# Gates and output projections of a second block by tokens, and a wide first FFN product, in an ordered two-block kernel

## The chip, the cores and the metric

One core of one Trainium2 chip runs the whole program. The metric is the device time of one execution in microseconds (us), the median over several runs.

## The reference

Two blocks of a network on 256 tokens of width 1024, in fp32. The first block (a state-space mixer, a latent attention, a convolutional FFN) is not touched but by the order of its instructions. The second block, cut to what matters:

```python
def second_block(x, ...):
    h = _rmsnorm(x, norm1_g)
    proj = h @ w_in                       # 1024 -> queries, keys, values, gates
    ... g_ma, g_mb = split(proj)          # 2 x 1024 gate columns, last in w_in
    y_a = _nsa_mixer(...)                 # 256 x 768: compressed, selected, window attention
    y_b = _dilated_mixer(...)             # 256 x 256
    mixed = sigmoid(g_ma) * (y_a @ w_o_a) + sigmoid(g_mb) * (y_b @ w_o_b)
    x = x + mixed @ w_out
    h2 = _rmsnorm(x, norm2_g)
    return x + jnp.square(jax.nn.relu(h2 @ w_up)) @ w_down   # 1024 -> 4096 -> 1024
```

Inside `_nsa_mixer`, `_compress` multiplies blocks of keys and of values (45 rows each) with two 2048x256 weights, 4 MB in all.

## The kernel before

**Products.** Each fp32 operand is split into a high part (a copy of type fp32r) and a low part (the rest), and a product is three matmuls that add up in PSUM: high x high, high x low, low x high. The helper's comments don't name it, so: in tile names `h` and `l` at the end are these parts. Weights stream from HBM in blocks of up to 128x2048. `need` (L319) issues for each half of a block a DMA on SyncE's queue into `wraw` (3 buffers), a ScalarE copy to `whi` and a VectorE subtraction to `wlo` (5 buffers each).

There are two forms of product. `pairB` (L502, with `mmB` L481) works by channels: a 128x128 weight is the stationary operand, the 256 tokens move, and the result has channels on the partitions; one matmul has 256 columns, a PSUM tile `pb` holds two channel blocks. `chunkA` (L491, with `mmA` L470) works by tokens: 128 tokens of the activation are stationary, 384 or 512 columns of weight move, the result `pa` has tokens on the partitions, one PSUM tile for each half of the tokens. Both take their PSUM from the tag `acc` (3 banks).

**Activations.** The stationary side needs channels on the partitions, so after each norm `norm_T` scales the rows (`xn` on VectorE) and `gain_T` (L423) transposes them on TensorE, 128x128 at a time, into a bank `trn`, two token halves per bank, and splits each bank into high and low with the gain as a scale (ScalarE, then VectorE). `late_T` (L442) does the same without the row scale, which is applied later. `spread` (L457) turns a column of row scales into a row `rrow` across channels, with two transposes `trr`.

**Second block.** In `block2` (L1291) the order of the text is: norm and transposes, the input product by tokens, queries and keys, compression (`kps` times `cw` weights into `ph`, 64 matmuls of 256 columns for keys and for values together, and the low parts `wlo` on 45 rows), attention, then the gates: eight `pairB` tiles, times `rrow` on VectorE, tanh on ScalarE (`tg`). Then `oa` (L1707): four `pairB` tiles over the 768 columns of `yAT`, gated into `mixA`; then `ob` over `yBT`, gated into `mixB`, added, and split into `mixT`. `out` is a product by tokens. The last FFN is 16 `pairB` tiles `up2`, relu on ScalarE (`r2`), square on VectorE (`u2`), split into `uT`, and two `chunkA` products over `uT` into the output.

**Order.** Nothing runs in the order of the text. `_Plan` (L655) records every operation, estimates its time with `_cost` (L575), simulates the engines and queues (a DMA by three constants) and picks what comes next on each engine by a rank: the table `RANK` (L41) gives each stage one number or one for each of its parts. A replay (L637) then issues everything in the order found, all from one line, L652 in the profile. So a change of a cost moves instructions everywhere, in the first block too.

```python
        if eng == "D":
            return max(150.0, 1.422 * n)
...
                elif e == "D":
                    end = now + 475.0
                    link = max(link, now + 1100.0) + ops[i][1][e]
                    fin = link + 700.0
```

Of the kernel before, what the change touches and what calls it, by code (L numbers as in the profile page):

```python
# [10 lines left out]
F32R = mybir.dt.float32r  # L11
# [6 lines left out]
P = 128  # L18
# [27 lines left out]
    "gate": [19.55, 0.24, 0.53, 11.34, -1.8, 19.33, 8.91, 19.47], "mix": [30],  # L46
    "in2": [39.8, 45.14, 45.06, 55.07, 49.45], "cmp": [40.9], "nsa": [41.09, 41.19, 49.84], "qb": [46.71, 41.14],
    "kb": [45.22, 46.76], "vb": [40.89, 41.09], "dil": [60.1, 50.29, 45.27, 41.14],
    "gate2": [46.76, 60, 62.18, 59.1, 60, 60.05, 45.57, 54.81], "mix2": [70, 70, 70, 71, 72], "ffn2": [80]}
PASSES = 3  # L50
# [26 lines left out]
def _weights():  # L77
# [33 lines left out]
    for nm, c0, n in A2_CHUNKS:  # L111
        for i in range(2):
            add((nm, i), 4 * n, "w_in_2", lambda w, i=i, c0=c0, n=n: _blk(w, range(4 * i, 4 * i + 4), [(c0, n)]))
        if nm == "qa1":
            for kv in "kv":
                for i in range(2):
                    add(("cw", kv, i), 2048, "cmp_%s_w1_2" % kv, lambda w, i=i: _blk(w, range(8 * i, 8 * i + 8), [(0, 256)]))
    for i in range(8):
        add(("g2", i), 2048, "w_in_2", lambda w, i=i: _tiles(w, (2 * i, 2 * i + 1), range(8), GA2))
    for i in range(4):  # L120
        add(("oa", i), 1536, "w_o_a_2", lambda w, i=i: _tiles(w, (2 * i, 2 * i + 1), range(6)))
    add(("ob", 0), 2048, "w_o_b_2", lambda w: _tiles(w, range(8), range(2)))
    for n in range(2):
# [18 lines left out]
def _cut(key, w):  # L142
    return 768 if key[0] == "mla" else w // 2

# [138 lines left out]
def _body(plan, x_in, wts, cst, out):  # L283
# [35 lines left out]
    def need(key):  # L319
        o, w = woff[key]  # L320
        src = wts[o:o + P * w].rearrange("(p n) -> p n", p=P)
        cut = _cut(key, w)
        parts = []
        plan.block = key
        for a, b in ((0, cut), (cut, w)):
            raw = plan.tile("wts", [P, 1024], F32, "wraw", "wraw", WRAW)
            plan.fetch = len(plan.ops)
            DQ.dma_start(raw[:, :b - a], src[:, a:b])
            hi = plan.tile("wts", [P, 1024], F32R, "whi", "whi", WHL)
            lo = plan.tile("wts", [P, 1024], F32R, "wlo", "wlo", WHL)  # L330
            A.activation(hi[:, :b - a], raw[:, :b - a], AF.Copy)
            V.tensor_tensor(lo[:, :b - a], raw[:, :b - a], hi[:, :b - a], op=OP.subtract)
            parts.append((a, hi, lo))
        plan.block = None
        return parts

    def wsl(w, o, n):
        a, hi, lo = w[1] if o >= w[1][0] else w[0]
        return hi[:, o - a:o - a + n], lo[:, o - a:o - a + n]
# [82 lines left out]

    def gain_T(xs, gain, name):  # L423

        res = hl(name, 4)
        for k in range(8):
            ps = ps_tr("trn")[:, :T]
            for tt in range(NTT):
                PE.transpose(ps[:, tt * P:(tt + 1) * P], xs(tt, k), ident)
            split((res[k // 2][0][:, k % 2], res[k // 2][1][:, k % 2]), ps, gain[:, k:k + 1])  # L430
        return res
# [9 lines left out]

    def late_T(x, gain, name):  # L442

        plan.rank, back = ("first", 0), plan.rank
        res = gain_T(lambda tt, k: x[:, tt, k * P:(k + 1) * P], gain, name)
        plan.rank = ("norm", 0)
# [78 lines left out]
class _Plan:  # L525
# [49 lines left out]
    def _cost(eng, op, outs, ins):  # L575
# [3 lines left out]
        if eng == "D":  # L579
            return max(150.0, 1.422 * n)  # L580
        if eng == "PE":
# [11 lines left out]
        if op == "tensor_tensor_reduce":  # L593
            outs = outs[:1]
        if eng == "A":
            return 0.833 * n + (51.0 if psum else 93.0) + 93.0 * (ptr + len(outs) - 1)
        fast = op in ("tensor_scalar", "tensor_copy", "memset") and not psum
        return (0.52 if fast else 1.042) * n + 68.0 + 61.0 * ptr

# [105 lines left out]
    def _run(self, graph, seq):  # L705
# [29 lines left out]
        while done < n:  # L735
# [23 lines left out]
            for e in ENGS:  # L759
# [45 lines left out]
                elif e == "D":  # L805
                    end = now + 475.0
                    link = max(link, now + 1100.0) + ops[i][1][e]
                    fin = link + 700.0
                else:
# [481 lines left out]
def block2(env, x2):  # L1291
# [31 lines left out]
    V.tensor_scalar(rnh, rn, 0.5, None, op0=OP.mult)  # L1323
    rrow = S.spread(rnh)

# [120 lines left out]
    for kv in range(2):  # L1446
        kps = []
        pos = C("pos" + "kv"[kv])
        for s0 in range(4):
# [7 lines left out]
            kps.append(t)  # L1457
        for i in range(2):
            w = S.need(("cw", "kv"[kv], i))
            for j in range(8):  # L1460
# [6 lines left out]
                if last:  # L1467
                    PE.matmul(ph[:90, c], both, wh, start=False, stop=True)
    hp = a2("hp")[:90]
    S.copy(hp, ph[:90])  # L1470
# [163 lines left out]
    for hp in range(2):  # L1634
# [28 lines left out]
        for i in range(2):  # L1663
# [3 lines left out]
            for b, n in enumerate((384, 512, 256)):  # L1667
                tt = min(b, 1)
                S.copy(prob[i][b][:, :n], prob[i][b][:, :n], rd[:, tt:tt + 1])
        pTs = []  # L1670
        for g in range(3):
            pT = S.pt_tile("pT3")
            o = (g % 2) * 256
            for i in range(2):
# [3 lines left out]
                S.copy(pT[:, i], pt[:, :384])  # L1678
            pTs.append(pT)
        po = ps_o("pob")[:, :T]  # L1680
        S.plan.group = ("pob", hp)
        for g in range(3):
            for kb in range(2):
                for i in range(2):
                    hd = 4 * g + 2 * hp + i
                    PE.matmul(po[64 * i:64 * i + 64, kb * P:], vb[hd // 6][kb][:, (hd % 6) * 64:(hd % 6) * 64 + 64],
                              pTs[g][:, i, 2 * kb * P:(2 + kb) * P], start=g == 0 and kb == 0, stop=g == 2 and kb == 1)
        S.plan.group = None
        S.split((yBT[0][0][:, hp], yBT[0][1][:, hp]), po)


    tg = []
    for i in range(8):
        S.rank("gate2", i)
        ps = S.pairB(("g2", i), hT)
        t = a2("tg").rearrange("p (a b) -> p a b", a=2)
        V.tensor_tensor(t, ps, rrow[:, None, :].to_broadcast([P, 2, T]), op=OP.mult)
        A.activation(t, t, AF.Tanh)
        tg.append(t)
    mixA = []  # L1700
    for i in range(4):
        S.rank("mix2", i)
        ps = S.pairB(("oa", i), yAT, 6)
        t = a2("mixA").rearrange("p (a b) -> p a b", a=2)
        V.scalar_tensor_tensor(t, tg[i], 1.0, ps, op0=OP.add, op1=OP.mult)
        mixA.append(t)
    mixT = S.hl("mixT", 4)  # L1707
    S.rank("mix2")
    w = S.need(("ob", 0))
    for i in range(4):  # L1710
        ps = S.ps_acc("pob2").rearrange("p (a b) -> p a b", a=2)
        for m in range(2):
            S.mmB(ps[:, m], yBT, w, 2, lambda k: ((2 * i + m) * 2 + k) * P)
        t = a2("mixB").rearrange("p (a b) -> p a b", a=2)
        V.scalar_tensor_tensor(t, tg[4 + i], 1.0, ps, op0=OP.add, op1=OP.mult)
        V.tensor_tensor(t, t, mixA[i], op=OP.add)
        S.split(mixT[i], t)
    x3 = x2
# [8 lines left out]
    S.rank("ffn2")  # L1727
    hT, ms = S.late_T(x3, C("g_n2"), "hT")
    rsq = small("rsq", 2)
    V.reciprocal(rsq, ms)  # L1730
    uT = S.hl("uT", 16)
    for i in range(16):
        ps = S.pairB(("up2", i), hT)
        t = a2("u2").rearrange("p (a b) -> p a b", a=2)
        r = a2("r2").rearrange("p (a b) -> p a b", a=2)
        A.activation(r, ps, AF.Relu)
        V.tensor_tensor(t, r, r, op=OP.mult)
        S.split(uT[i], t)
# [42 lines left out]
```

## Time and profile before

| | |
|---|---|
| median of 3 runs | 995.23 us (994.27 to 995.67) |
| own time of the profiled execution | 995.55 us |
| its span in the trace | 993.8 us |
| mean granted TensorE clock | 0.993 of full speed |
| HBM read | 164.18 MB, 166 GB/s over the span |

The span runs from the first to the last recorded instruction; 1.75 us of the execution's own time lie around it. TensorE is PE in the rows (its weight loads PEld), VectorE DVE, ScalarE ACT, SyncE SP. A row's duration of a pipelined matmul overlaps that of the next, so what one costs is read from start to start, or from the length of a chain of many. `A<-B,C` means that tile A is written from B and C.

### The profile page before, as it was taken

The numbers are of one execution on the slowest core, as the hardware profiler recorded it, in microseconds if no ns is written. First come the engines' busy times: TensorE is split into PE (matmuls) and PEld (weight loads), VectorE is DVE, ScalarE is ACT, GpSimd is POOL, SyncE is SP. The second block draws the span as 40 slices with busy tenths as digits, with TensorE's granted clock in tenths as the row PEclk, the third lists the DMA queues.
The fourth block names the chain that finished last, engine by engine and source line by source line (L and its number), as shares of the span: only waits on it lengthen the run. The fifth ranks groups of instructions, "written<-read, shape, count | busy, mean of one in ns | idle before, by whom it ended". The sixth has DMA issues, their size and how long they took to land.

```text
span 993.8 us, 18122 instructions
## 1 busy us (share of the span) xinstructions
PE 979.3 (99%) x6737; PEld 906.7 (91%) x6737; DVE 787.0 (79%) x1841; ACT 615.2 (62%) x1233; POOL 0.2 (0%) x4
## 2 busy tenths in 40 slices
PE   9999999999999999999999998999999999999998
PEld 7899988999999899999988997998889989998886
DVE  6887999999787779989954999999877866665442
ACT  6665889877554566666653666867676455554341
POOL 0000000000000000000000000000000000000000
PEclk9999999999999999999999998999999999999999
DMA  7655644344455555555565555534323556555561
GB/s 253 221 168 163 211 128 164 101 132 156 148 172 180 174 181 185 187 178 186 186 198 158 172 167 188 186 114 131 125 91 113 183 181 198 178 182 187 188 218 64
DMA packets 50537, 166.44 MB, mean 167 GB/s; under 512 B 5617, under 2 KB 6929, under 8 KB 50321
## 3 DMA queue, kind: packets, MB, share of 16 engines
q1 hardware_dynamic: 50448, 165.28, 51.3%
q8 instruction: 53, 0.87, 0.4%
q14 instruction: 36, 0.29, 0.1%
HBM read 164.18 MB, written 1.08 MB: 166 GB/s over the span
## 4 chain that ended last, share of the span: by engine, by line
PE 88%; DVE 5%; DMA 4%; ACT 2%; issue 1%; SPq 0%; DVEq 0%; ACTq 0%
PE pb L652 46%; PE pa L652 28%; DMA wraw<-in_wts_dram 4%; DVE wlo L652 2%; PE trp L652 2%; PE py L652 1%; ACT whi L652 1%; PE po L652 1%; PE psS L652 1%; PE pob L652 1%; PE pq L652 1%; PE trq L652 1%; PE pov L652 1%; PE pk L652 1%; PE psN L652 1%
## 5 line engine op out<-in xcount | busy, mean ns | idle before, releaser
L652 DVE TENSOR_TENSOR wlo<-wraw,whi 128x1024 fp32r<-128x1024 f32 (+3 forms) x318 | 368.2, 1161 | 160.0 <-ACT whi L652 156.4
L652 ACT ACTIVATE whi<-wraw 128x1024 fp32r<-128x1024 f32 (+3 forms) x318 | 320.9, 1010 | 276.2 <-PE pb L652 146.2
L652 PE MATMUL pb<-hTl,whi 128*128 128x256 f32 x1056 | 302.3, 287 | 0.0
L652 PE MATMUL pb<-hTh,wlo 128*128 128x256 f32 x1056 | 302.2, 287 | 0.0
L652 PE MATMUL pb<-hTh,whi 128*128 128x256 f32 x1056 | 301.6, 286 | 0.0
L652 PEld LDWEIGHTS pb<-hTl,whi 128*128 128x128 f32 x1056 | 203.6, 193 | 2.1 <-issue 1.9
L652 PEld LDWEIGHTS pb<-hTh,wlo 128*128 128x128 f32 x1056 | 203.7, 193 | 1.3 <-issue 1.0
L652 PEld LDWEIGHTS pb<-hTh,whi 128*128 128x128 f32 x1056 | 203.6, 193 | 1.0 <-issue 0.8
L652 PE MATMUL pa<-whi,uTh 128*128 128x512 f32 x216 | 84.2, 390 | 0.0
L652 PE MATMUL pa<-whi,uTl 128*128 128x512 f32 x216 | 84.2, 390 | 0.0
L652 PE MATMUL pa<-wlo,uTh 128*128 128x512 f32 x216 | 84.2, 390 | 0.0
L652 PE MATMUL pa<-whi,hTh 128*128 128x384 f32 (+2 forms) x224 | 80.5, 361 | 0.0
L652 PE MATMUL pa<-whi,hTl 128*128 128x384 f32 (+2 forms) x224 | 79.7, 356 | 0.0
L652 PE MATMUL pa<-wlo,hTh 128*128 128x384 f32 (+2 forms) x224 | 79.4, 355 | 0.0
L652 PEld LDWEIGHTS pa<-whi,uTl 128*128 128x128 f32 x216 | 40.6, 188 | 8.5
L652 PEld LDWEIGHTS pa<-wlo,uTh 128*128 128x128 f32 x216 | 40.6, 188 | 8.3
L652 PEld LDWEIGHTS pa<-whi,uTh 128*128 128x128 f32 x216 | 40.6, 188 | 8.2
L652 PEld LDWEIGHTS pa<-whi,hTh 128*128 128x128 f32 x224 | 42.2, 189 | 2.3 <-issue 0.3
L652 PEld LDWEIGHTS pa<-whi,hTl 128*128 128x128 f32 x224 | 42.1, 188 | 2.3 <-issue 0.3
L652 PEld LDWEIGHTS pa<-wlo,hTh 128*128 128x128 f32 x224 | 42.2, 189 | 2.0 <-issue 0.2
L652 PE MATMUL pb<-ysTh,wlo 128*128 128x256 f32 x128 | 37.0, 289 | 0.0
L652 DVE SCALAR_TENSOR_TENSOR fcv<-fpr,call,fcv 128x254 f32<-128x254 f32 (+1 forms) x88 | 36.6, 478 | 0.3 <-ACT fcv L652 0.3
(396 smaller groups left out, 1724.6 us busy)
## 6 DMA issues: line engine op xcount, KB each, us to landing
wraw<-in_wts_dram SPq DMA_DIRECT2D x250, 512.0 KB, 4.2
wraw<-in_wts_dram SPq DMA_DIRECT2D x52, 384.0 KB, 3.2
dec<-aD SPq DMA_DIRECT2D x16, 256.0 KB, 5.9
wraw<-in_wts_dram SPq DMA_DIRECT2D x8, 256.0 KB, 2.7
wraw<-in_wts_dram SPq DMA_DIRECT2D x4, 448.0 KB, 4.4
wraw<-in_wts_dram SPq DMA_DIRECT2D x4, 420.0 KB, 3.9
call<-in_cst_dram SPq DMA_DIRECT2D x1, 1076.5 KB, 9.1
out_dram<-yo SPq DMA_DIRECT2D x3, 256.0 KB, 4.0
```

Source lines behind the costliest of these rows:

```text
L652: getattr(engines[eng], op)(*[swap(a) for a in args], **{k: swap(a) for k, a in kw.items()})
```

## The change

The gates become four `chunkA` products of 512 columns; tanh reads PSUM directly with the row scale as its scale operand, so `rrow` and its `spread` go. `ob` and `oa` become `chunkA` products per half of the output columns; the gated sum `mixB` has tokens on the partitions and is turned by 16 transposes `trm`, two channel blocks per bank, then split into `mixT`. In the last FFN, `gain_T` keeps each of the eight channel blocks as one tile with the high part beside the low part; a high weight then multiplies both in one matmul of 512 columns, and the low weight multiplies the high part in one of 256, into PSUM tiles `pu` of another tag (`g`, 5 banks). ScalarE or VectorE copies the second half to `l2`, VectorE adds it to the first (`u2`) and does relu and square in one operation. In `gain_T` two channel blocks share a bank: four transposes, then two splits. The `pob` matmuls of the dilated attention stand with their group's transposes instead of after all groups. In the planner the constants of a DMA and of half-height operations change, and some ranks.

```diff
-    "gate2": [46.76, 60, 62.18, 59.1, 60, 60.05, 45.57, 54.81], "mix2": [70, 70, 70, 71, 72], "ffn2": [80]}
+    "gate2": [46.76, 60, 60, 54.81], "mix2": [70, 70.2, 70.1, 71, 72], "ffn2": [80]}
...
-            return max(150.0, 1.422 * n)
+            return max(150.0, 1.8 * n)
...
+        half = 115.0 if n >= 256 and outs[0].ap[0][1] == 64 else 0.0
...
-                    end = now + 475.0
-                    link = max(link, now + 1100.0) + ops[i][1][e]
-                    fin = link + 700.0
+                    end = now + 430.0
+                    link = max(link, now + 1000.0) + ops[i][1][e]
+                    fin = link + 1060.0
...
         for k in range(8):
-            ps = ps_tr("trn")[:, :T]
-            for tt in range(NTT):
-                PE.transpose(ps[:, tt * P:(tt + 1) * P], xs(tt, k), ident)
-            split((res[k // 2][0][:, k % 2], res[k // 2][1][:, k % 2]), ps, gain[:, k:k + 1])
+            if k % 2 == 0:
+                pair = ps_tr("trn").rearrange("p (a b) -> p a b", a=2)
+                for tt in range(NTT):
+                    for j in range(2):
+                        PE.transpose(pair[:, j, tt * P:(tt + 1) * P], xs(tt, k + j), ident)
+            ps = pair[:, k % 2]
+            dst = (res[k][:, 0], res[k][:, 1]) if beside else (res[k // 2][0][:, k % 2], res[k // 2][1][:, k % 2])
+            split(dst, ps, gain[:, k:k + 1])
...
-    rrow = S.spread(rnh)
...
-        ps = S.pairB(("g2", i), hT)
-        t = a2("tg").rearrange("p (a b) -> p a b", a=2)
-        V.tensor_tensor(t, ps, rrow[:, None, :].to_broadcast([P, 2, T]), op=OP.mult)
-        A.activation(t, t, AF.Tanh)
-        tg.append(t)
...
+    for n in range(4):
+        S.rank("gate2", n)
+        ps = S.chunkA([("g2", n, 0), ("g2", n, 1)], hT, 512, 4)
+        tg.append([a2("tg") for _ in range(NTT)])
+        for tt in range(NTT):
+            A.activation(tg[n][tt], ps[tt], AF.Tanh, scale=rnh[:, tt:tt + 1])
+    mixT = []
+    for n in range(2):
+        S.rank("mix2", n)
+        mix = [a2("mixB") for _ in range(NTT)]
+        ps = S.chunkA([("ob", n)], yBT, 512, 2)
+        for tt in range(NTT):
+            V.scalar_tensor_tensor(mix[tt], tg[2 + n][tt], 1.0, ps[tt], op0=OP.add, op1=OP.mult)
+        ps = S.chunkA([("oa", n, 0), ("oa", n, 1)], yAT, 512, 3)
+        for tt in range(NTT):
+            t = a2("mixA")
+            V.scalar_tensor_tensor(t, tg[n][tt], 1.0, ps[tt], op0=OP.add, op1=OP.mult)
+            V.tensor_tensor(mix[tt], t, mix[tt], op=OP.add)
+        S.rank("mix2", 2 + n)
+        mixT += S.hl("mixT", 2)
+        for i in range(2):
+            pt = ps_tr("trm").rearrange("p (a b) -> p a b", a=2)
+            for j in range(2):
+                for tt in range(NTT):
+                    PE.transpose(pt[:, j, tt * P:(tt + 1) * P], mix[tt][:, (2 * i + j) * P:(2 * i + j + 1) * P], ident)
+            S.split(mixT[2 * n + i], pt)
...
-        ps = S.pairB(("up2", i), hT)
         t = a2("u2").rearrange("p (a b) -> p a b", a=2)
-        r = a2("r2").rearrange("p (a b) -> p a b", a=2)
-        A.activation(r, ps, AF.Relu)
-        V.tensor_tensor(t, r, r, op=OP.mult)
+        l = a2("l2").rearrange("p (a b) -> p a b", a=2)
+        w = S.need(("up2", i))
+        for m in range(2):
...
+            ps = ps_o("pu").rearrange("p (a b) -> p a b", a=2)
+            for k in range(8):
+                wh, wl = S.wsl(w, (m * 8 + k) * P, P)
+                PE.matmul(ps, wh, hT[k], start=k == 0, stop=False)
+                PE.matmul(ps[:, 0], wl, hT[k][:, 0], start=False, stop=k == 7)
+            S.copy(l[:, m], ps[:, 1])
+            V.tensor_tensor(t[:, m], ps[:, 0], l[:, m], op=OP.add)
+        V.scalar_tensor_tensor(t, t, 0.0, t, op0=OP.max, op1=OP.mult)
         S.split(uT[i], t)
```

The weights of these products are packed to match (`_weights` L77): blocks of 2048 columns for the gates, 1536 for `oa`, 1024 for `ob`, and `_cut` (L142) loads `oa` as 1024 and 512 columns and `ob` whole. The number of DMAs on SyncE stays at 353.

How instructions move is shown at three places. The first is VectorE at the head of the program, where the norm of the latent queries begins (`xres` is the input, `xn` its scaled rows, `call` a tile of constants). Before:

```order
L652 TENSOR_SCALAR rnh<-ny 128x2
L652 TENSOR_SCALAR xn<-xres,ny 128x512 x2
L652 TENSOR_TENSOR wlo<-wraw,whi 128x1024
L652 TENSOR_SCALAR xn<-xres,ny 128x512
L652 TENSOR_TENSOR wlo<-wraw,whi 128x1024
L652 TENSOR_SCALAR xn<-xres,ny 128x512
L652 TENSOR_TENSOR wlo<-wraw,whi 128x1024
```

After:

```order
L665 TENSOR_SCALAR rnh<-ny 128x2
L665 TENSOR_SCALAR xn<-xres,ny 128x512 x4
L665 TENSOR_SCALAR m_292<-ss_277 128x1
L665 COPY mcaus<-call 128x128
L665 TENSOR_TENSOR ropet_298<-call 128x64
...
L665 TENSOR_TENSOR kra<-qkv,ropet_305 128x32
L665 SCALAR_TENSOR_TENSOR hTl<-trn,call,hTh 128x256 x3
L665 TENSOR_TENSOR krb<-qkv,ropet_309 128x32
L665 TENSOR_TENSOR wlo<-wraw,whi 128x1024
```

All four scalings now stand together, ahead of the weight parts that stood between them.

The second is TensorE at the compression, at the first matmul of `ph` (`psN` are scores of the window and selected attention, `pa` a chunk of the input product). Before:

```order
L652 MATMUL ph<-whi,kps 90x256
L652 MATMUL psN<-kTh,qT_7544 128x256
L652 MATMUL psN<-kTl,qT_7544 128x256
L652 MATMUL psN<-kTh,qT_7544 128x512
L652 MATMUL ph<-wlo,kps 45x256
L652 MATMUL ph<-whi,kps 90x256
L652 MATMUL pa<-whi,hTh 128x384
```

After:

```order
L665 MATMUL ph<-whi,kps 90x256
L665 MATMUL psN<-kTh,qT_7509 128x256
L665 MATMUL psN<-kTl,qT_7509 128x256
L665 MATMUL psN<-kTh,qT_7509 128x512
L665 MATMUL psN<-kTl,qT_7509 128x512
L665 MATMUL pa<-whi,hTh 128x384
L665 MATMUL pa<-wlo,hTh 128x384
L665 MATMUL pa<-whi,hTl 128x384
```

The chunk of 24 `pa` matmuls stood behind the first `wlo` matmul of `ph`, and now stands ahead of it.

The third is TensorE where the mixing passes into the product `out`. Before:

```order
L652 MATMUL pb<-yATl,whi 128x256
L652 MATMUL pb<-yATh,wlo 128x256
L652 MATMUL pa<-whi,mixTh 128x512
L652 MATMUL pa<-wlo,mixTh 128x512
L652 MATMUL pa<-whi,mixTl 128x512
```

After (with the numbers of the tiles, since two products and two `mixB` alternate):

```order
L665 MATMUL pa_9831<-whi_9775,mixTl_9816 128x512
L665 MATMUL trm_9855<-call_74,mixB_9800 128x128
L665 MATMUL trm_9857<-call_74,mixB_9800 128x128
L665 MATMUL pa_9861<-whi_9727,mixTh_9796 128x512
...
L665 MATMUL pa_9861<-whi_9775,mixTl_9816 128x512
L665 MATMUL trm_9855<-call_74,mixB_9820 128x128
L665 MATMUL trm_9855<-call_74,mixB_9800 128x128
L665 MATMUL trm_9855<-call_74,mixB_9820 128x128
L665 MATMUL trm_9857<-call_74,mixB_9820 128x128
```

The transposes of `mixB` now stand between pieces of the product `out`, nine matmuls after the first two of them.

## Rows read from the trace of the kernel before

**Rows 1.** The page: busy shares, and the chain that ended last by engine.

```profile
PE 979.3 (99%) x6737; PEld 906.7 (91%) x6737; DVE 787.0 (79%) x1841; ACT 615.2 (62%) x1233; POOL 0.2 (0%) x4
...
PE 88%; DVE 5%; DMA 4%; ACT 2%; issue 1%; SPq 0%; DVEq 0%; ACTq 0%
```

**Rows 2.** The chain in order of time: start us, us, what.

```profile
514.28 0.87 PE trn L652 x8
...
812.66 90.31 PE pb L652 x752
902.97 87.08 PE pa L652 x384
```

**Rows 3.** Stretches: us, busy (x instructions) of PE, PEld, DVE, ACT, POOL, clock, DMA share, GB/s.

```profile
44.00:48.00 4.00, 3.39 (x16) 3.42 (x17) 4.00 (x11) 2.40 (x5) 0.00 (x0) 0.58 0.52 189
597.00:618.00 21.00, 17.14 (x98) 14.66 (x97) 19.55 (x51) 14.43 (x22) 0.00 (x0) 0.84 0.54 179
597.00:611.00 14.00, 11.25 (x74) 9.66 (x72) 13.22 (x38) 7.81 (x11) 0.00 (x0) 1.00 0.54 188
611.00:618.00 7.00, 5.89 (x24) 5.01 (x25) 6.33 (x14) 6.62 (x12) 0.00 (x0) 0.52 0.53 163
640.00:990.00 350.00, 349.60 (x2381) 318.81 (x2379) 239.70 (x542) 191.25 (x345) 0.00 (x0) 1.00 0.49 156
813.00:903.00 90.00, 90.00 (x751) 90.00 (x750) 57.93 (x69) 49.11 (x66) 0.00 (x0) 1.00 0.57 186
```

**Rows 4.** Timelines of TensorE, then VectorE, 21 to 45 us: start us, us, what.

```profile
21.94 1.18 PE L652 MATMUL trn<-call,xn 128*128 128x128 f32 x8 [0.43 <-DVE xn L652]
...
41.87 0.28 PE L652 MATMUL pb<-hTl,whi 128*128 128x256 f32 x1
44.61 0.44 PE L652 MATMUL trl<-call,qn 128*128 128x128 f32 x1 [2.46 <-DVE qn L652]
...
23.23 0.48 DVE L652 TENSOR_SCALAR xn<-xres,ny 128x512 f32<-128x512 f32 x1
23.63 1.23 DVE L652 TENSOR_TENSOR wlo<-wraw,whi 128x1024 fp32r<-128x1024 f32 x1
...
42.97 1.23 DVE L652 TENSOR_TENSOR wlo<-wraw,whi 128x1024 fp32r<-128x1024 f32 x1
44.11 1.00 DVE L652 TENSOR_SCALAR qn<-qkv,ny 128x256 f32<-128x256 f32 x4
```

**Rows 5.** Timeline of TensorE, 598 to 615 us: the rows with waits over 0.3 us.

```profile
598.52 0.32 PE L652 MATMUL ph<-wlo,kps 128*45 128x256 f32 x1 [0.82 <-DVE wlo L652]
...
601.72 0.41 PE L652 MATMUL trq<-call,qrot 128*128 128x128 f32 x2 [0.33 <-DVE qrot L652]
...
608.11 0.35 PE L652 MATMUL ph<-whi,kps 128*90 128x256 f32 x1 [0.34 <-ACT whi L652]
609.37 0.32 PE L652 MATMUL ph<-wlo,kps 128*45 128x256 f32 x1 [0.91 <-DVE wlo L652]
...
611.55 0.44 PE L652 MATMUL ph<-wlo,kps 128*45 128x256 f32 x1 [0.91 <-DVE wlo L652]
...
614.47 0.58 PE L652 MATMUL psN<-kTh,qT 128*128 128x256 f32 x1 [0.55 <-ACT pr L652]
```

**Rows 6.** Timeline of VectorE where it runs without a pause, three places.

```profile
106.83 0.42 DVE L652 COPY vtok<-pk 128x256 f32<-128x256 f32 x1
107.16 0.42 DVE L652 COPY ktok<-pk 128x256 f32<-128x256 f32 x1
...
405.32 0.42 DVE L652 TENSOR_TENSOR sg<-sg,fcv 128x256 f32<-128x256 f32 x1
405.65 0.68 DVE L652 TENSOR_TENSOR fpr<-pb,rrow 128x512 f32<-128x512 f32 x1
...
782.23 0.68 DVE L652 TENSOR_TENSOR mixTl<-mixB,mixTh 128x512 fp32r<-128x512 f32 x1
782.83 0.68 DVE L652 TENSOR_TENSOR mixB<-mixB,mixA 128x512 f32<-128x512 f32 x1
```

## What the change will do to the time

> **What bounds the kernel now.** I read the page's shares first: TensorE is busy for 979.3 of 993.8 us and the chain that ended last is 88% TensorE [rows 1]. That says which engine, not what one matmul costs; a matmul's own duration overlaps its neighbours. So the next view is the chain in order of time. In the last layer 752 matmuls of 256 columns stand there as one piece of 90.31 us, 120.1 ns each, and 384 of 512 columns as 87.08 us, 226.8 ns each; eight transposes take 0.87 us, 0.109 each [rows 2]. The step from 256 to 512 columns is 106.7 ns, so 13.4 ns of every matmul don't depend on its width. In both pieces TensorE waits for nothing: there only less TensorE work helps.
>
> Third, the table of stretches, to see where TensorE does wait. From 640 to 990 its busy time is the whole stretch but for 0.4 us. Two places stand out [rows 3]: 44 to 48 us (16 matmuls in 4 us, granted clock 0.58) and 597 to 618 (17.14 busy of 21.0, of which 611 to 618 ran at 0.52). The timeline names the waits. In the first, a transpose of `qn` waits 2.46 us for VectorE [rows 4]. In the second, six waits sum to 3.9 us: three for a weight part (`wlo` twice 0.91, once 0.82), one 0.34 for `whi`, two for other work [rows 5]. After each cluster the clock sits at the lower of its levels, 1.2 of 2.4 GHz, for some us: 4 us at 0.58 lose 1.7 us, 7 us at 0.52 lose 3.4.
>
> **Term 1, matmuls: -5.8 us.** All counts come from the order of instructions on TensorE. Last layer: 16 tiles x 2 x 8 steps x 3 matmuls of 256 columns (768) become 256 of 512 and 256 of 256: 768 x 0.1201 = 92.2; 256 x 0.2268 + 256 x 0.1201 = 88.8; -3.4. Gates: 384 of 256 become 192 of 512: 46.1 to 43.5, -2.6. Output projections (144 + 48 of 256 become 72 + 24 of 512): 23.1 to 21.8, -1.3. The products by tokens must be turned back: 16 transposes of `mixB` more, 2 of `rcol` fewer, 14 x 0.109 = +1.5. All of it is on the path, as [rows 2, 3] show no other cover there.
>
> A rule speaks against this term. The trace has 13.4 ns of fixed cost per matmul, read at two widths in streams without waits [rows 2]. The Trainium skill (TensorE: Matmul & The Clock Gate, Back-to-back issue gap) gives a full-clock matmul N/2.4 ns plus about 2.5. By that rule 544 fewer matmuls save 1.4 us, the transposes eat it, and term 1 would be about 0 (an estimate). The trace disagrees by 10.9 ns per matmul at both widths, so I keep -5.8.
>
> **Does VectorE keep up in the last layer?** Per tile it now does two weight parts, two copies and two additions of 256 columns from PSUM, the squared relu and the low part (the plan gives 2 of the 32 copies to ScalarE). Spacings in back-to-back stretches: 1.14 us for 1024 columns, 0.60 for 512, 0.33 for a copy of 256 from PSUM, 0.34 for an operation on two tensors of 256 [rows 4, 6]. Sum 2.28 + 1.20 + 0.67 + 0.68 = 4.8 us against 16 pairs of matmuls of 0.347 = 5.55 us of TensorE. Today it is 2.28 + 1.20 = 3.5 of 48 x 0.1201 = 5.77 us (the row from 813 to 903 has 57.93 of 90 busy) [rows 3]. So it goes from 60% to 87%: cost nothing, but with 0.7 us of cover per tile. Five PSUM banks turn over every 2.8 us, so the extra hop isn't a wait.
>
> **Term 2, the head: -2.8 us (-4.2 to +0.5).** The planner's costs of a load and of half-height operations change, so the whole order is made anew. VectorE now scales all four `xn` before the next weight part (today weight parts stand between them), and `qn` comes after 7 weight parts of 1024 columns instead of 11 (counted in the order). Today the eleventh holds `qn` until 44.11 [rows 4], because that part's load and copy are late. Without it TensorE gains up to 2.46 + 0.43 (the wait for `xn`) + 1.7 of clock = 4.6, less what is late next: weight loads, which now start behind `xn`. An `xn` takes 0.40 us (23.23 to 23.63) [rows 4], so the weight parts shift by 2 to 3 us; stepping through the new order I estimate `qn` ready near 37.5 and TensorE asking for it near 37. So I leave 1.8 us of waits and clock, 0.4 to 4.6 being possible, and take 2.8 as gained. The bound of +0.5 is the same wait in another place, and a little longer.
>
> **Term 3, the compression stage at 597 to 618: -0.5 us (-3 to +3).** 24 matmuls of a chunk now run between the first `ph` and its `wlo` partner, which removes the 0.82 wait. But the weights stay as they are: four blocks of 1 MB serve 64 matmuls of some 0.12 us, 7.7 us together, while loads moved 188 GB/s there [rows 3], 22 us for 4 MB. That shortage is filled by other work or waited for, in either plan. Both ends come from [rows 3, 5]: half of the 7.3 us lost may go, or as much may come.
>
> **Term 4, late attention and mixing: +0.2 us (-1 to +1).** The gates lose 8 VectorE operations of 512 columns (4.8 us), where VectorE isn't the bound. At the end of the mixing a new chain appears: product, two VectorE operations, transposes, split, next product. From the last attention product to the first matmul that needs the last `mixTl`, VectorE has 14 operations of 0.60 and 5 weight parts of 1.14, 14.4 us with the split of `yBT`; TensorE has 73 matmuls and 16 transposes, 18.3 us. Stepping through both orders with these spacings, the transposes find `mixB` ready by about 0.2 us each time. Tight, not late.
>
> Two transposes-per-bank in the norms: the same transposes, in groups of four as today; the filler around them stays. 0.
>
> **Sum.** 995.55 (this execution; 993.8 of span) - 5.8 - 2.8 - 0.5 + 0.2 = 986.65; that execution is 0.32 above the median of 995.23, so **986.4 us** against the median.
>
> **Rivals.**
> 1. *The new order gains nothing where TensorE waits.* Head at +0.5 and compression at +2: 995.2 - 5.8 + 2.5 + 0.2 = 992.1. For it: a plan removes a wait only where its costs are right, and the shortage of weights stays. Against: `qn` plainly stands earlier. 0.15.
> 2. *Wide matmuls save little.* If one of 512 columns costs two of 256, term 1 is only +1.5, and the time 995.2 + 1.5 - 3.1 = 993.6; if the fixed part is a fifth of the 13.4 ns (2.7), a fifth of the 7.3 saved is 1.5, term 1 is 0, and the time 992.1. Against both speak two widths, in this same kernel [rows 2]. 0.03 together. The rule of the Trainium skill above is close to the second.
> 3. *VectorE becomes the bound in the last layer.* If every hand-over between the engines adds 0.2 us to its 4.8 (six per tile), a tile takes 6.0 instead of 5.55, 16 x 0.45 = 7.2 us: 993.6. Against: today's spacings hold right beside ScalarE's hand-overs. 0.05.
> 4. *Slower: the mixing chain stalls TensorE and its clock falls.* There are four joins (two groups of transposes for each half). If VectorE is late at each as at the head, 2.46 us and 1.7 us of clock [rows 3, 4], that is 16.6 us: 1003. It decides from three joins on (12.5 us, more than the 8.9 gained and the 2 of the bound). For it: the slack is 0.2 us and VectorE's order is fixed. Against: lateness at the first join is partly made up, and matmuls of the next product stand between. 0.06.
>
> The rest, 0.71, is the forecast, 982.5 to 990.
>
> **How the numbers follow.** The best ends of terms 2 to 4 give 995.2 - 5.8 - 4.2 - 3 - 1 = 981.2, the worst 995.2 - 5.8 + 0.5 + 3 + 1 = 993.9; that all three end on one side is rare, so the range goes from 982 to 992, which leaves out rival 4, most of rivals 2 and 3, half of rival 1 and the lowest corner: some 0.2. About 0.2% (2 us) is what a measurement can tell from no change. Faster by that means under 993.2: the forecast 0.71, most of rival 1 and parts of 2 and 3: 0.86. Within 0.2%: 0.08. Slower: rival 4, 0.06.
>
> **What would show it.** Right: the last layer's first product as one piece of 88.8 us, its VectorE busy share near 0.87 by spacing; no wait for `qn` over 1 us and a clock near 1.00 from 44 to 48; 544 fewer matmuls wider than a transpose; lost time at `ph` of 5 to 9 us. Wrong: pieces of 512 columns over 230 ns each, waits for `u2` or `l2` by TensorE, or a clock under 0.9 where `trm` runs.

## The result, and the profile after the change

| | before | the change |
|---|---|---|
| median | 994.04 us (989.81 to 995.67, 6 runs) | 983.59 us (982.61 to 988.12, 6 runs) |
| ratio | | 0.990 (95% interval 0.9881 to 0.9918) |
| profiled execution, span | 993.8 us | 980.8 us |

The change is faster by about 1%: 986.4 against 995.2, a ratio of 0.991, had been forecast. Measured once more on another occasion (run c_change below) the ratio is 0.9921 (0.9903 to 0.994).

The page's shares, to be held against [rows 1]:

```profile
PE 968.3 (99%) x6207; PEld 871.6 (89%) x6207; DVE 801.3 (82%) x1884; ACT 610.9 (62%) x1227; POOL 0.2 (0%) x4
```

TensorE has 530 instructions fewer (544 matmuls fewer, 14 transposes more) and 11.0 us less busy time; the span is 13.0 us shorter. Busy time counts matmuls at the lower clock at their full length, so this doesn't yet say how much of it is work. The chain in order of time shows the last layer, as [rows 2] did:

```profile
802.71 0.44 PE trn L665 x4
803.15 86.84 PE pu L665 x501
889.99 87.08 PE pa L665 x384
```

501 records in 86.84 us are 0.1733 each, 88.7 us for all 512; the same product took 768 x 0.1201 = 92.2 before. The stretches that answer to [rows 3] (columns as there):

```profile
36.00:44.00 8.00, 8.00 (x67) 7.76 (x66) 7.24 (x17) 5.45 (x9) 0.00 (x0) 1.00 0.65 217
44.00:48.00 4.00, 4.00 (x36) 4.00 (x35) 3.81 (x7) 2.76 (x4) 0.00 (x0) 1.00 0.64 223
597.00:612.00 15.00, 11.05 (x71) 9.01 (x70) 14.14 (x41) 11.10 (x19) 0.00 (x0) 0.89 0.59 193
770.00:790.00 20.00, 20.00 (x99) 16.53 (x99) 15.57 (x20) 10.34 (x14) 0.00 (x0) 1.00 0.48 160
803.00:890.00 87.00, 87.00 (x504) 76.09 (x503) 81.01 (x129) 43.07 (x55) 0.00 (x0) 1.00 0.59 193
```

From 36 to 48 us TensorE is now busy throughout at a clock of 1.00; before, 44 to 48 ran at 0.58. The compression (597 to 612) still idles for 4 us at a clock of 0.89. The mixing with its transposes (770 to 790) has no idle time. VectorE is busy 81 of 87 us in the last layer's first product, where it was 58 of 90. The timelines of TensorE, then VectorE, answer to [rows 4 to 6]:

```profile
36.27 0.50 PE L665 MATMUL trl<-call,qn 128*128 128x128 f32 x2
37.91 0.64 PE L665 MATMUL trl<-call,qn 128*128 128x128 f32 x4
...
591.44 0.28 PE L665 MATMUL ph<-whi,kps 128*90 128x256 f32 x1
...
603.58 0.32 PE L665 MATMUL ph<-wlo,kps 128*45 128x256 f32 x1 [1.73 <-DVE wlo L665]
606.02 0.44 PE L665 MATMUL ph<-wlo,kps 128*45 128x256 f32 x1 [0.51 <-DVE wlo L665]
...
611.40 0.32 PE L665 MATMUL ph<-wlo,kps 128*45 128x256 f32 x1 [0.69 <-DVE wlo L665]
...
770.75 0.38 PE L665 MATMUL trm<-call,mixB 128*128 128x128 f32 x2
...
781.48 0.82 PE L665 MATMUL trm<-call,mixB 128*128 128x128 f32 x6
...
976.66 0.39 PE L665 MATMUL pa<-whi,uTl 128*128 128x512 f32 x1
```

```profile
35.87 0.45 DVE L665 TENSOR_SCALAR qn<-qkv,ny 128x256 f32<-128x256 f32 x2
...
820.69 0.42 DVE L665 COPY l<-pu 128x256 f32<-128x256 f32 x1
821.15 0.42 DVE L665 TENSOR_TENSOR u<-pu,l 128x256 f32<-128x256 f32 x1
```

`qn` is scaled at 35.87 instead of 44.11, and its transposes wait for nothing. `ph` still waits for `wlo` three times, 2.93 us in sum (2.64 before). No `trm` waits. The whole neighbourhood of the compression, 585 to 625 us, in before, the change and c_change:

```profile
585.00:625.00 40.00, 36.15 (x212) 33.11 (x212) 38.19 (x107) 27.28 (x49) 0.00 (x0) 0.91 0.56 176
585.00:625.00 40.00, 36.05 (x228) 32.73 (x227) 38.70 (x122) 32.09 (x69) 0.00 (x0) 0.96 0.59 188
585.00:625.00 40.00, 36.54 (x219) 33.93 (x218) 38.55 (x118) 29.82 (x60) 0.00 (x0) 0.91 0.62 185
```

In the last layer, a copy whose result the next operation reads starts 0.46 us before it, where [rows 6] have 0.33.

**Where the time came from.** Three starts on TensorE cut every execution into stretches that the experiments share: A from the start to the first `ph`, B from there to the last transposes `trn` (compression, attention, gates, mixing), C from there to the last matmul. In us:

| profiled execution | A | B | C |
|---|---|---|---|
| before | 596.95 | 215.11 | 177.59 |
| the change | 591.44 | 211.11 | 174.11 |
| c_change, the change again | 594.35 | 211.39 | 175.74 |
| e1_costs | 592.30 | 215.40 | 177.57 |
| e8_dma_only | 591.60 | 217.39 | 177.57 |
| e2_old_costs | 598.43 | 215.05 | 174.11 |
| e3_ffn_only | 596.46 | 213.65 | 177.65 |
| e10_ffn_paired | 596.94 | 216.37 | 174.13 |
| e4_narrow | 594.60 | 210.68 | 177.51 |
| e5_unpaired | 592.45 | 210.85 | 177.64 |
| e11_no_ffn | 594.45 | 209.66 | 177.58 |
| e6_dve1 | 595.22 | 213.27 | 174.13 |
| e7_dve2 | 593.97 | 209.74 | 175.73 |
| e12_late | 593.27 | 209.73 | 175.73 |

A and B scatter by up to 4 us between executions whose orders there are the same (the change, c_change, e4_narrow, e11_no_ffn, e6_dve1, e7_dve2, e12_late); C takes a few values only, which repeat to 0.1 us. The change gains 5.5, 4.0 and 3.5 us in its first profile. A row is one execution: that of e2_old_costs is the slowest of its eleven, that of e8_dma_only the fastest of its twelve.

### The profile page after: what moved, and what is told of

The parts are those of the page before. It is cut to its first block, busy times and chain, and to the rows that moved or that the text cites. A ratio compares the mean times of both kernels' runs of the same rounds, so it can differ in the third digit from the quotient of the medians.

```text
span 980.8 us, 17142 instructions
## 1 busy us (share of the span) xinstructions
PE 968.3 (99%) x6207; PEld 871.6 (89%) x6207; DVE 801.3 (82%) x1884; ACT 610.9 (62%) x1227; POOL 0.2 (0%) x4
## 5 line engine op out<-in xcount | busy, mean ns | idle before, releaser
L665 PE MATMUL pb<-hTl,whi 128*128 128x256 f32 x672 | 191.5, 285 | 0.0
L665 PE MATMUL pb<-hTh,whi 128*128 128x256 f32 x672 | 191.0, 285 | 0.0
L665 PE MATMUL pb<-hTh,wlo 128*128 128x256 f32 x672 | 190.9, 284 | 0.0
L665 PEld LDWEIGHTS pb<-hTh,wlo 128*128 128x128 f32 x672 | 128.9, 192 | 0.5 <-issue 0.5
L665 PEld LDWEIGHTS pb<-hTl,whi 128*128 128x128 f32 x672 | 128.7, 192 | 0.6 <-issue 0.5
L665 PEld LDWEIGHTS pb<-hTh,whi 128*128 128x128 f32 x672 | 128.7, 192 | 0.3 <-issue 0.2
L665 PE MATMUL pu<-hTk,whi 128*128 128x512 f32 x256 | 88.8, 394 | 0.0
L665 PE MATMUL pu<-hTk,wlo 128*128 128x256 f32 x256 | 70.9, 278 | 0.0
L665 PEld LDWEIGHTS pu<-hTk,whi 128*128 128x128 f32 x256 | 47.9, 188 | 11.0
L665 PEld LDWEIGHTS pu<-hTk,wlo 128*128 128x128 f32 x256 | 48.1, 188 | 0.1
```

The source lines that it names most:

```text
L665: getattr(engines[eng], op)(*[swap(a) for a in args], **{k: swap(a) for k, a in kw.items()})
```

## The experiments

**The planner's constants.** e1_costs is the kernel before with these lines and the grouping of the `pob` matmuls (without which the planner finds no order):

```diff
-            return max(150.0, 1.422 * n)
+            return max(150.0, 1.8 * n)
...
+        half = 115.0 if n >= 256 and outs[0].ap[0][1] == 64 else 0.0
...
-                    end = now + 475.0
-                    link = max(link, now + 1100.0) + ops[i][1][e]
-                    fin = link + 700.0
+                    end = now + 430.0
+                    link = max(link, now + 1000.0) + ops[i][1][e]
+                    fin = link + 1060.0
...
-        S.plan.group = ("pob", hp)
+            S.plan.group = ("pob", hp, g)
```

> The kernel before with the change's planner constants (loads, half-height operations) and its grouping of the pob matmuls, which the planner needs to find an order with them; no product is changed. VectorE's order at the head becomes that of the change (all four xn together, qn four weight parts earlier). Theory (the wait for qn came from the order): the 2.5 us wait and the low clock behind it go, the granted clock from 44 to 48 us is 1.00, and the kernel is 4 to 6 us faster than before. Rival (the head lost its wait because of the new products or by a luckier arrival of weights): within 1.5 us of before, a wait of over 1 us for qn or for a weight part near 38 to 46 us. The compression stage loses 5 to 9 us by either.

Measured: ratio 0.9954 (0.9942 to 0.9967), 4.6 us faster. The wait for `qn` is down to 0.2 us, and the stretch 40 to 48 us of its trace has no idle time:

```profile
40.00:48.00 8.00, 8.00 (x69) 8.00 (x68) 7.16 (x15) 5.58 (x9) 0.00 (x0) 1.00 0.62 208
```

All of it lies in A (4.65 us in the profiles); B is as before. The theory holds. e8_dma_only leaves the half-height term out:

```diff
-        half = 115.0 if n >= 256 and outs[0].ap[0][1] == 64 else 0.0
```

> The kernel before with the planner's constants of a load alone and the grouping of the pob matmuls; the half-height term stays out. VectorE's order at the head is that of the change. Theory (the constants of a load move qn): 4 to 5.5 us faster than before, no wait for qn over 1 us, clock 1.00 from 44 to 48 us, as with both constants. Rival (the half-height term does it, or the grouping): within 1.5 us of before.

Measured: ratio 0.999 (0.9978 to 1.0002), no difference: the time is the rival's. Its trace has what the theory asked for at the head (a wait of 0.30 us for `qn`, clock 1.00, A at 591.60), and loses 2.3 us in B. So the constants of a load free the head in this execution, and the plan without the half-height term seems to give it back later; the 2.3 us lie within the scatter of B, the median lies another 1.7 us above this execution, and where the time goes stays open. e2_old_costs is the reverse: the change with the constants of before.

```diff
-            return max(150.0, 1.8 * n)
+            return max(150.0, 1.422 * n)
...
-        half = 115.0 if n >= 256 and outs[0].ap[0][1] == 64 else 0.0
...
-                    end = now + 430.0
+                    end = now + 475.0
```

> The change with the planner constants of before; all its new products stay. qn comes after one weight part fewer than before, not four. Theory: the matmul terms remain (5 to 6 us) and little of the head, 1 us or so: 6 to 7 us faster than before, with a wait for qn of 1 to 2.5 us in the trace. Rival (the gain is the planner's): 0 to 2 us faster.

Measured: ratio 0.9976 (0.9966 to 0.9986), 2.4 us faster: a miss for the theory, and 0.4 above the rival's range. In its profile C has its 3.5 us. B has nothing, though 2.4 us of matmuls are gone from it, and A is 1.5 longer. TensorE's waits (us in total, times, longest) name the new ones:

```profile
PE ph L664 <- DVE wlo L664: 2.8, 4, 1.0
PE trk L664 <- DVE ktok L664: 2.1, 1, 2.1
PE trl L664 <- DVE qn L664: 1.4, 1, 1.4
PE pkc L664 <- ACT pT L664: 1.3, 1, 1.3
PE trpc L664 <- ACT pr L664: 1.3, 2, 0.9
```

`trk` lies in A, `pkc` and `trpc` (compressed attention) in B. The profiles speak for gates and projections that need a plan whose costs fit: in e1_costs the constants alone bring nothing in B, in e2_old_costs the products alone bring nothing, and the eight profiles with both have B at 210.8 in the mean, against 215.6 for the five with neither or with the constants only. The times don't show it: 4.6 us for the constants and 2.4 for the products make 7.0, and the change measured again is 7.9 us faster (6.0 to 9.7), so that the two may as well just add up.

**The wide product of the last FFN.** e3_ffn_only is before with that product alone (the last hunks of the diff, `gain_T` with one channel block per bank):

```diff
+            ps = ps_o("pu").rearrange("p (a b) -> p a b", a=2)
...
+                PE.matmul(ps, wh, hT[k], start=k == 0, stop=False)
+                PE.matmul(ps[:, 0], wl, hT[k][:, 0], start=False, stop=k == 7)
```

> The kernel before with the last layer's first product alone changed (256 matmuls of 512 and 256 of 256 columns for 768 of 256; transposes one channel block per bank; old constants). Theory (13.4 ns of every matmul don't depend on its width): 3.4 us faster, the product takes 88.8 us instead of 92.2, and TensorE waits for nothing in it. Rival (about 2.5 ns): 0.6 us faster, the product takes 91.6. The wait for qn stays at about 2.5 us.

Measured: ratio 1.0 (0.9987 to 1.0012), no gain: a miss for the theory. The time doesn't exclude the rival's 0.6 us, but C is 177.65 as before, where the theory asks for 174.2 and the rival for 177.0. e4_narrow cuts the wide matmul in the change:

```diff
-                PE.matmul(ps, wh, hT[k], start=k == 0, stop=False)
-                PE.matmul(ps[:, 0], wl, hT[k][:, 0], start=False, stop=k == 7)
+                PE.matmul(ps[:, 0], wh, hT[k][:, 0], start=k == 0, stop=False)
+                PE.matmul(ps[:, 0], wl, hT[k][:, 0], start=False, stop=k == 7)
+            for k in range(8):
+                wh, wl = S.wsl(w, (m * 8 + k) * P, P)
+                PE.matmul(ps[:, 1], wh, hT[k][:, 1], start=k == 0, stop=k == 7)
```

> The change with each 512-column matmul of the last layer's first product cut into two of 256; all else is the same (tiles, banks, the copy and the addition). Theory (13.4 ns per matmul): the product takes 92.2 us again, 3.4 longer than in the change, and the kernel is 6 to 7 us faster than before instead of 9.9. Rival (2.5 ns): 0.6 longer than in the change, 9.3 faster than before. If the hand-over to VectorE cost anything in the change, that would show here as a product longer than 92.2.

Measured: ratio 0.9938 (0.9924 to 0.9951), 6.2 us faster than before, as the theory has it. Its chain shows the product:

```profile
805.88 90.24 PE pu L665 x752
```

That is 0.1200 us for each of 768, 92.2 in all, so the hand-over to VectorE costs nothing. C is 177.51, 3.40 longer than in the change, for 256 matmuls more: 13.3 ns each. Against c_change, an execution of the same program that is told of below, it is 1.77 longer, 6.9 ns each. The Trainium skill (TensorE: Matmul & The Clock Gate, Back-to-back issue gap) gives about 2.5 ns beside the columns for an isolated matmul at full clock; the prediction read it as that of a stream. For 256 matmuls that would be 0.6 us (an estimate), and neither comparison bears it out. So the width is worth what was said in the first profile, and something in e3_ffn_only eats it. Its product runs at 0.3533 us per pair of matmuls instead of 0.3467, and begins with a wait. Two runs ask whether the wait comes from the transposes' banks: e10_ffn_paired adds the change's `gain_T` to e3_ffn_only, e5_unpaired takes it out of the change:

```diff
-            ps = ps_tr("trn")[:, :T]
+            if k % 2 == 0:
+                pair = ps_tr("trn").rearrange("p (a b) -> p a b", a=2)
```

> The run of the FFN part alone, with the norms' transposes two channel blocks per bank as in the change (old constants, old gates and projections). From the last transposes of xres to the end the kernel before took 177.6 us, the change 174.1, and the run of the FFN part alone 177.6: it lost 1.3 us waiting for xres and hTk at the start, and its pairs of matmuls took 0.3535 us instead of 0.3467. Theory (the start's wait comes from single-block banks): that stretch takes 174 to 175 us and the kernel is 2.5 to 3.5 us faster than before. Rival (the wait comes from the order that the old constants make): the stretch stays at 177 and the kernel within 1 us of before.

> The change with the norms' transposes one channel block per bank, as before. Prediction's step (pairing costs and saves nothing): 9 to 11 us faster than before, as the change. Rival (pairing is what keeps the start of the last FFN free of waits): 1.5 to 3.5 us slower than the change, with a wait of 0.9 us or more for hTk at the start of the last FFN.

Measured: e10_ffn_paired 0.9985 (0.9973 to 0.9998), C at 174.13 and its product without a wait; e5_unpaired 0.9932 (0.9919 to 0.9946), C at 177.64 with a wait of 0.98 us for `hTk`. By C and the waits the theory holds in the first and the rival in the second. The times say less: e10_ffn_paired is 1.5 us faster than before, not 2.5 to 3.5 (in its profile B is 1.3 us above that of before); and the intervals don't part e5_unpaired (6.8 us faster) from the change measured again. TensorE's timeline of e5_unpaired at the start of the product:

```profile
801.48 0.39 PE L661 MATMUL pu<-hTk,whi 128*128 128x512 f32 x1
...
802.75 0.28 PE L661 MATMUL pu<-hTk,wlo 128*128 128x256 f32 x1
803.30 0.66 PE L661 MATMUL trn<-call,xres 128*128 128x128 f32 x4 [0.27 <-DVE xres L661]
804.94 0.73 PE L661 MATMUL pu<-hTk,whi 128*128 128x512 f32 x2 [0.98 <-DVE hTk L661]
```

The order of TensorE there, with the numbers of the tiles, tells what is waited for:

```
L661 MATMUL pu_10063<-hTk_10001,wlo_9976 128x256
L661 MATMUL trn_10044<-call_74,xres_82 128x128
L661 MATMUL trn_10046<-call_74,xres_82 128x128
L661 MATMUL trn_10048<-call_74,xres_82 128x128
L661 MATMUL trn_10050<-call_74,xres_82 128x128
L661 MATMUL pu_10097<-hTk_9985,whi_10006 128x512
L661 MATMUL pu_10063<-hTk_10085,whi_9964 128x512
```

`pu` and `trn` share a tag of five banks. With one channel block per bank the last four transposes hold four of them, and one tile of `pu` (10063) is open. Its eight matmuls that can run stand ahead; the next, into a second tile (10097), reads an `hTk` that was there long before, and waits until the split of a `trn` frees a bank. With two blocks per bank `trn` holds two, and three tiles of `pu` are open: in the change eleven matmuls stand ahead of the transposes and nine behind, before one needs a new `hTk`. The two runs show that pairing removes the wait. At the same pace, from the first `pu` to the last, the product takes 92.47 us in e5_unpaired and 90.71 in c_change, so the wait with what surrounds it costs 1.8 us. (C says 1.90, but 0.5 of that is three matmuls that stand ahead of the cut in c_change, and the wait of 0.27 for `xres` lies ahead of it.) That it is the banks is read from this order. e11_no_ffn has the last FFN of before within the change:

```diff
-    hT, ms = S.late_T(x3, C("g_n2"), "hT", True)
+    hT, ms = S.late_T(x3, C("g_n2"), "hT")
...
+        ps = S.pairB(("up2", i), hT)
```

> The change with the last FFN's first product as before (768 matmuls of 256 columns). Theory (the parts add up once the new constants are in): 3.5 us slower than the change, 6 to 7 faster than before, the stretch from the last transposes to the end at 177.6 us. Rival (the FFN's gain depends on the rest or the rest on it): more than 1.5 us off that, to either side.

Measured: ratio 0.9936 (0.9918 to 0.9954), 6.4 us faster than before, C at 177.58, as the theory has it.

**VectorE's cover.** e6_dve1 and e7_dve2 put one and two operations more into each tile (their value is unchanged):

```diff
+        V.tensor_tensor(t, t, t, op=OP.max)
         V.scalar_tensor_tensor(t, t, 0.0, t, op0=OP.max, op1=OP.mult)
```

> The change with one more VectorE operation of 512 columns in each of the 16 tiles of the last FFN (the maximum of u2 with itself, which leaves its value). By the prediction's sum (4.8 us of VectorE per tile against 5.55 of TensorE) it is 5.4 and costs nothing. By the trace of the change a copy that the next operation reads takes 0.46 us instead of 0.33, so that a tile needs about 5.05, with the added operation 5.65 to 5.8: TensorE would wait for PSUM, and the kernel be 1.5 to 4 us slower than the change. TensorE's order is that of the change.

> The change with two more VectorE operations of 512 columns in each of the 16 tiles of the last FFN. One more left the stretch from the last transposes to the end at 174.1 us. By the prediction's sum VectorE needs 4.8 + 1.2 = 6.0 us per tile against 5.55 of TensorE: the 16 tiles take 7 us longer, 181 us for the stretch. By the trace's 5.05 per tile it is 6.25 and 11 us, 185. If it stays at 174 the sum for VectorE is wrong and there is more cover than 0.7 us.

Measured: e6_dve1 0.9925 (0.9908 to 0.9942), C at 174.13: the added operation is free, as the prediction's sum had it. Its stretch of the product, and VectorE's timeline in it:

```profile
809.00:896.00 87.00, 87.00 (x503) 76.04 (x503) 85.47 (x142) 44.69 (x55) 0.00 (x0) 1.00 0.59 194
...
842.68 0.42 DVE L665 TENSOR_TENSOR u<-pu,l 128x256 f32<-128x256 f32 x1
843.13 0.69 DVE L665 TENSOR_TENSOR u<-u 128x512 f32<-128x512 f32 x1
843.74 0.42 DVE L665 COPY l<-pu 128x256 f32<-128x256 f32 x1
844.08 0.68 DVE L665 SCALAR_TENSOR_TENSOR u<-u 128x512 f32<-128x512 f32 x1
```

The plan put another operation between the copy and the addition that reads it, so the copy is back at 0.34 us (843.74 to 844.08), and one more copy went to ScalarE. The second forecast fell with its premise of 0.46.

e7_dve2 0.9904 (0.988 to 0.9927), C at 175.73, which is that of c_change (175.74): two are free as well, against both forecasts. The stretch 810 to 885 us of e7_dve2, and its ScalarE group for `l2` there (busy us, mean ns, idle before):

```profile
810.00:885.00 75.00, 75.00 (x426) 65.07 (x425) 74.36 (x116) 38.91 (x54) 0.00 (x0) 1.00 0.58 190
...
L665 ACT ACTIVATE l<-pu 128x256 f32<-128x256 f32 x15 | 5.5, 366 | 1.8 <-PE pu L665 1.8
```

VectorE is busy 74.36 of 75 us, and TensorE still doesn't wait: the planner gave some half of the copies of `l2` to ScalarE, which is busy only half of the time. So neither run held the rest fixed; they show that the real cover is VectorE's and ScalarE's together, and that the order matters to it.

**The pace of the product.** c_change is the change itself, with no edit.

> The change itself, once more, against the kernel before on one chip. The parts measured so far (costs of the planner and the grouping of pob -4.6 us; from there to the change without the wide FFN product another -1.9; the wide FFN product with paired transposes -3.5 by its stretch) give 9 to 11 us faster. If the first profile of the change was a lucky execution, 7 to 9.

Measured: ratio 0.9921 (0.9903 to 0.994), 7.9 us faster, in the range that was given for a lucky first profile. Its wait for `qn`, and its chain:

```profile
PE trl L665 <- DVE qn L665: 1.1, 1, 1.1
...
806.34 88.42 PE pu L665 x501
894.77 87.11 PE pa L665 x384
```

The same program, the same 501 records, 1.58 us more than in the first profile. So one order with the same places of tiles runs at 0.3467 us per pair in one execution and at 0.3533 in another. e12_late was made to test whether a wait at the start sets it:

```diff
             split(dst, ps, gain[:, k:k + 1])
+            if beside and k in (4, 5):
+                for _ in range(4):
+                    A.activation(dst[0], dst[0], AF.Copy)
```

> The change with four more ScalarE copies of each of two hTk tiles (k = 4 and 5) onto themselves, so that the last FFN's first product has to wait once for hTk while the rest of the order stays. In the two runs with unpaired transposes the whole product ran at 0.3535 us per pair of matmuls instead of 0.3467, after a wait of 1.0 us for hTk. If a wait at the start sets that pace, the pairs take 0.3535 here too and the stretch is 1.7 us longer than the wait alone makes it; if not, the pairs take 0.3467 and only the wait (about 1 us) is added to the 174.1 of the stretch.

Measured: ratio 0.9902 (0.9882 to 0.9922), C at 175.73 at 0.3533 us per pair. TensorE doesn't wait for `hTk` in it, as other matmuls stand ahead, so the test did not take place; but the pace came without a wait, as in c_change. Of nine profiles with the wide product four have 0.3467 (the change, e2, e10, e6) and five 0.3533 (e3, e5, c_change, e7, e12). The five are the two without pairing, which wait at the start, and the three that ran together on the chip of c_change, which don't. Whether the chip or the occasion sets the pace was not tested; what sets it is open.

## Why the prediction was right, step by step

- **The sum, -8.8.** The measured 10.4 us and, again, 7.9 lie on either side of it. That is in part luck: the constants gain 4.6 us by themselves (e1_costs) where 2.8 stood for the head, and in executions at the other pace the last layer gains 1.85 of its 3.4. The terms as written give 986.3, not 986.4.
- **Fixed cost per matmul, last layer -3.4.** Right in the first profile: C is 3.48 us shorter, and e4_narrow returns 3.40. That a stream of two widths can run at two paces no row of before could tell.
- **Gates and projections -2.4 with their transposes.** Not shown by themselves: no run has these products alone under the new constants. B came out 4.0 shorter, but it scatters by 3.6 at one order and holds the compression too. e11_no_ffn, which differs from e1_costs by these products, their ranks and the pairing, is 6.4 us faster than before against 4.6: 1.8 more, near the 2.4, with intervals that overlap. That a fitting plan may be a condition was not in the prediction: the profile of e2_old_costs has the same matmuls and no gain in B.
- **Head -2.8.** The mechanism was right (`qn` behind fewer weight parts, wait and clock gone), the size too small for the first profile (5.5 in A). Over the ten profiles with the new constants of a load A is 593.4 in the mean (591.4 to 595.2), over the four without 597.2 (596.5 to 598.4): 3.8 us. The first profile of the change was a favourable execution; c_change has an A of 594.35 and a wait of 1.1 us for `qn`, over the 1 us that the prediction had set as a sign. The 1.8 us left for waits was near what such executions show.
- **Compression -0.5.** Right within its range: the 0.82 wait went, another grew to 1.73, and the waits for `wlo` stayed within 0.3 us in sum. From 585 to 625 us idle time and clock together lose 7.5 us before, 5.6 in the first profile of the change and 7.1 in c_change, within the 5 to 9 that the prediction had set; that is 1.9 and 0.4 us gained.
- **Mixing +0.2.** Right that no join is late; all `trm` run without a wait at a clock of 1.00, so rival 4 did not come.
- **"Two transposes-per-bank in the norms ... 0."** This step failed in its reason. The change has the pairing, so the sum is not hurt, but it looked at the transposes and not at the banks that they hold: without pairing, the start of the last FFN loses 1.8 us (the product of e5_unpaired 92.47 against 90.71 at the same pace). The -3.4 rests on it.
- **VectorE at 87% of the product.** By spacing it was about 5.05 of 5.55 us, 91%, because a copy that is read at once takes 0.46 us (its busy share is 93%, where before it was 64% and the spacing had said 60%). That it costs nothing was right, and there is more room than 0.7 us, as the plan parts the copy from its reader and ScalarE takes copies over.

## What to carry to other kernels

Where one engine is the bound and its stream has no waits, count instructions and read the cost of one from the spacing at two widths: that sum held at one of the two paces, and half of it at the other. Price a change of tiling together with the PSUM banks that it holds while the next stage wants to begin, and with the plan that orders it: the same products gained 2.4 us under the old constants, and 3.3 or 5.8 on top of the new ones (7.9 or 10.4 less 4.6). And profile the same kernel more than once before a microsecond is explained.

## What was not expected of the hardware

A stream that alternates matmuls of 512 and 256 columns ran at 0.3467 us per pair in some executions and at 0.3533 in others, from its first 40 matmuls or so to its end and with the granted clock at 1.00 in both, while the streams of one width stayed at 87.08 to 87.12 us for 384 matmuls. And a VectorE operation that reads the result of the one just ahead of it starts 0.13 us later than one that doesn't (0.46 against 0.33 for a copy of 256 columns; 0.34 in e6_dve1, where another operation follows the copy).
